# Two-layer hybrid decoder step on one core: group b's rows loaded ahead of the fourth weight, and one scale-and-bias of the last norm on GpSimd

## The chip, the cores and the metric

One core of one Trainium2 chip runs the whole program. The metric is device microseconds (us) of one execution; a median of three runs is given, and one further execution was recorded by the hardware profiler. The engines are TensorE (PE; its weight loads are listed apart as PEld), VectorE (DVE), ScalarE (ACT), GpSimd (POOL) and SyncE (SP), which issues most DMAs.

## The reference, cut to what matters

```
def reference(...):
    for i in range(2):                       # two layers
        if i == 0:   # sliding-window attention, 16 heads, rotary positions, sinks
            mp, kp, vp = swa_prompt(xp, w_qkv, b_qkv, sinks, w_o)       # 512 prompt rows
            ms, ks, vs = swa_sample(xs, cache_k, cache_v, ...)          # 8 sample rows
        else:        # gated linear attention on a matrix state
            mp, sp = gla_mix(xp, zeros, ...); ms, ss = gla_mix(xs, state_gla, ...)
        xp = layer_norm(ALPHA * xp + mp, ln_mix_g[i], ln_mix_b[i])
        xs = layer_norm(ALPHA * xs + ms, ln_mix_g[i], ln_mix_b[i])
        fp = conv_ffn(xp, ...); fs = conv_ffn(xs, ...)   # (gelu(conv3(x W_a)) * (x W_u)) W_down
        xp = layer_norm(ALPHA * xp + fp, ln_ffn_g[i], ln_ffn_b[i])
        xs = layer_norm(ALPHA * xs + fs, ln_ffn_g[i], ln_ffn_b[i])

def layer_norm(x, g, b):
    mu = mean(x); var = mean((x - mu) ** 2)
    return (x - mu) * rsqrt(var + 1e-5) * g + b
```

All is float32, with d_model 1024, 512 prompt rows and 8 sample rows.

## The kernel before

Activations lie transposed: a row of the model (1024 features) is spread over 128 partitions in 8 chunks (`KD`). The rows are split into group a (256 prompt rows) and group b (the other 256 and the 8 samples, 264 columns). `g.x` is a group's residual; `g.xh` and `g.xl` (for group a both in `xs_a`) are the high and low part of its rows for TensorE.

A weight matrix is worked off in units of 128 output columns: `load_unit` has SP load a unit into a `raw` tile (512 KB; `RAWS` = 2 such tiles, so that a load waits until the split of the unit two before it is done), ScalarE rounds it to the high part `wh` (L196), VectorE subtracts to get the low part `wl` (L202). `product` then runs 24 matmuls for one unit and one group: for each of 8 chunks high by high (L238), high weight by low rows (L240), low weight by high rows (L242). In the trace the results are tiles `accp`.

Units 0 and 1 are the keys and values of the attention layer, units 2 to 9 the queries, two heads of the 16 in each. After a query's product follow the rotation (`rope`: ScalarE `ra`, VectorE `rb`, GpSimd twice, L572 to L578), the split into `hl` (L623, L624), four small DMAs that rearrange it to `qs` (L628), scores against the keys (`sc`, L656, L657), softmax (L666 to L679), two transposes (`tp`, L685), two triangular cuts on GpSimd (`pu`, `pl`, L691) and the product with the values (`pv`, L704). The score tiles `sc` have two buffers. Then come the output projection (`out_proj`) and the norm (`ln_chunk`, `ln_end`), the feed-forward part, and the second layer with the gated linear attention.

`load_x` loads rows of a group into `g.x` and splits them: `xh` on ScalarE (L315), `xl` on VectorE (L316), one instruction of each per chunk. `attn_open` issues all loads of the start. Its loads on SP are under a manual schedule, in the order in which they are written. The order of the instructions on the other engines, and of SP later on, is set by a scheduler that estimates times when the program is built (`schedule_with_timeline_sim=True`). Every engine then works its own list strictly in that order.

The last norm of a group (`ln_end` with `last`) first gets its two sums from matmuls (L381, L383), then a short row of small steps on ScalarE and VectorE (L391 to L414), then goes over the 8 chunks in four pairs: VectorE multiplies a pair by the reciprocal deviation (L423), and each chunk is scaled and shifted by its own parameters: chunks 0, 1, 2, 4 and 6 on ScalarE (L426), chunk 3 on GpSimd (L428), chunks 5 and 7 on VectorE (L430). SP stores a pair when both are done (L437); of the last pair of group b, SP stores chunk 7 (L434) and ScalarE's queue chunk 6 (L435). `issue_after(behind)` holds a pair's multiplication behind the VectorE scaling of the pair before.

Of the kernel before, what the change touches and what calls it, by code (L numbers as in the profile page):

```python
# [82 lines left out]
def parted(rows):  # L83

    return rows.rearrange("p (j t) -> p t j", t=2)
# [15 lines left out]
class Net:  # L101
# [274 lines left out]
    def ln_end(self, g, i, last=False):  # L376
        nc, n, x = self.nc, g.n, g.x
        yield 0 if g.i and not last else 1
        e1, e2 = self.mtile("tp")[:, :n], self.mtile("pv")[:, :n]
        for e, sums, rest in ((e1, g.s1, x[:, KD - 1]), (e2, g.s2, g.q)) if last else ((e1, g.s1, None), (e2, g.s2, None)):  # L380
            nc.tensor.matmul(e, self.ones_a, sums, start=True, stop=rest is None)  # L381
            if rest is not None:
                nc.tensor.matmul(e, self.ones_a, rest, start=False, stop=True)  # L383
        t = lambda name, b=1: self.ln.tile([P, NT - 256], F32, name=name, bufs=b)[:, :n]
        mu, q, nv, r = t("mu"), t("msq"), t("nv"), t("r")
        banks = last or i % 2 == 0
        if banks:

            nv, vr = self.mtile("sc")[:, :n], self.mtile("sc")[:, :n]
        if last:  # L390
            self.square = nc.scalar.activation(q, e1, AF.Square).ins  # L391
            with self.tc.issue_after(self.square):
                nc.scalar.copy(mu, e1)
            for m in range(2, KD):
                nc.gpsimd.tensor_tensor(x[:, m], x[:, m], mu, op=ALU.subtract)
        else:
            self.square = nc.scalar.activation(q, e1, AF.Square).ins
        nvi = nc.vector.scalar_tensor_tensor(nv, q, LN_EPS, e2, op0=ALU.subtract, op1=ALU.subtract)

        with self.tc.issue_after(nvi.ins):  # L400
            for m in range(0, 2 if last else KD, 2):
                xp = x[:, m:m + 2]
                nc.vector.tensor_tensor(xp, xp, e1.unsqueeze(1).broadcast_to([P, 2, n]), op=ALU.subtract)
        nc.scalar.activation(r, nv, AF.Ln, scale=-1.0)
        self.exp = nc.scalar.activation(r, r, AF.Exp, scale=-0.5).ins
        if banks:
            nc.vector.tensor_tensor(vr, nv, r, op=ALU.mult)
            q = nv
            nc.vector.scalar_tensor_tensor(q, vr, 0.5, r, op0=ALU.mult, op1=ALU.mult)
        else:  # L410
            nc.vector.tensor_tensor(q, r, r, op=ALU.mult)
            nc.vector.scalar_tensor_tensor(q, q, 0.5, nv, op0=ALU.mult, op1=ALU.mult)
        rp = e2
        nc.vector.scalar_tensor_tensor(rp, q, 1.5, r, op0=ALU.add, op1=ALU.mult)  # L414
        sc = lambda m: self.par[:, C_LNG + i * KD + m:C_LNG + i * KD + m + 1]
        bi = lambda m: self.par[:, C_LNB + i * KD + m:C_LNB + i * KD + m + 1]
        if last:

            behind = None
            for m in range(0, KD, 2):  # L420
                xp = x[:, m:m + 2]
                with self.tc.issue_after(behind) if behind else ExitStack():
                    nc.vector.tensor_tensor(xp, xp, rp.unsqueeze(1).broadcast_to([P, 2, n]), op=ALU.mult)  # L423
                for j in (m, m + 1):
                    if j in (0, 1, 2, 4, 6):
                        nc.scalar.activation(x[:, j], x[:, j], AF.Identity, scale=sc(j), bias=bi(j))  # L426
                    elif j == 3:
                        nc.gpsimd.tensor_scalar(x[:, j], x[:, j], sc(j), bi(j), op0=ALU.mult, op1=ALU.add)  # L428
                    else:
                        behind = nc.vector.tensor_scalar(x[:, j], x[:, j], sc(j), bi(j), op0=ALU.mult, op1=ALU.add).ins  # L430
                y = lambda m0, m1: self.O["y"][:, m0:m1, g.c0:g.c0 + n]
                if g.i and m == KD - 2:

                    nc.sync.dma_start(out=y(m + 1, m + 2), in_=x[:, m + 1:m + 2])  # L434
                    nc.scalar.dma_start(out=y(m, m + 1), in_=x[:, m:m + 1])  # L435
                else:
                    nc.sync.dma_start(out=y(m, m + 2), in_=xp)  # L437
            return

        for m in range(KD):  # L440
            v = nc.vector.scalar_tensor_tensor(x[:, m], x[:, m], sc(m), rp, op0=ALU.mult, op1=ALU.mult)
            nc.scalar.activation(g.xh[:, m], parted(x[:, m]), AF.Identity, bias=bi(m))
            xl = nc.vector.scalar_tensor_tensor(g.xl[:, m], parted(x[:, m]), bi(m), g.xh[:, m].bitcast(F32), op0=ALU.add, op1=ALU.subtract)
        self.rest = xl.ins
        if g.i == 0:
            self.norm = self.slot + HOLD, self.exp, v.ins, xl.ins, self.next_phase() + 1
        if i % 2 == 0:
            if g.i:
                self.spawn(self.row_sums(i), 1)
            return  # L450
        for m in range(KD):
            yield 1 if m else LATEB
            self.shift(g, i, m)
# [66 lines left out]
    def attn_open(self):  # L520
        nc, I = self.nc, self.I
        self.ap, self.ap_cm = self.open("attn")
        p = self.ap
        t = lambda s, name, dt=F32: p.tile(s, dt, name=name)
        self.rope_t = t([P, 2, NT], "rope_t")
        self.mask0 = t([P, P], "mask0")
        self.own = t([P, 2, P], "own", I32)


        warm = self.acc.tile([P, 512], F32, name="accp")  # L530
        for _ in range(WARM):
            nc.tensor.matmul(warm[:, :P], self.ones_a, self.ones_a, start=True, stop=True)
        with self.tc.manual_schedule(engines={mybir.EngineType.SP}):
            r = self.raw.tile([P, KD * P], F32, name="raw")
            h, l = (self.wts.tile([P, KD * P], F32R, name=n) for n in ("wh", "wl"))
            for m in range(0, KD, 4):
                c = slice(m * P, m * P + 4 * P)
                nc.sync.dma_start(out=r[:, c], in_=I["w_qkv"][0][:, c])
                nc.gpsimd.tensor_scalar(h[:, c], r[:, c], 1.0, 0.0, op0=ALU.mult, op1=ALU.add)
                self.load_x(0, m, m + 2)  # L540
                nc.vector.tensor_tensor(l[:, c], r[:, c], h[:, c].bitcast(F32), op=ALU.subtract)
                self.load_x(0, m + 2, m + 4)
            self.w[0] = (h, l)
            self.load_unit(1, 4)
            nc.sync.dma_start(out=self.par, in_=I["par"])
            nc.sync.dma_start(out=self.rope_t[:, :, 0:256], in_=I["rope"][:, :, 0:256])
            nc.sync.dma_start(out=self.ident, in_=I["ident"])
            self.load_unit(2, 2)
            self.load_unit(3)
            for m in range(0, KD, 4):  # L550
                self.load_x(1, m, m + 4)
            nc.sync.dma_start(out=self.rope_t[:, :, 256:], in_=I["rope"][:, :, 256:])
            nc.sync.dma_start(out=self.mask0, in_=I["mask"])
            nc.sync.dma_start(out=self.own, in_=I["own"])
            for i in range(4, WSLOTS):
                self.load_unit(i)
        self.bq = t([P, KD], "bq")
        nc.vector.tensor_scalar(self.bq, self.par[:, C_BQKV + 2:C_BQKV + 10], 0.125, None, op0=ALU.mult)
        self.khi = [t([P, SEQ], f"khi{v}", F32R) for v in range(2)]
        self.klo = [t([P, SEQ], f"klo{v}", F32R) for v in range(2)]  # L560
        self.vtok = t([P, 4, P], "vtok")
        self.kc = t([P, NS, P], "kc")
        self.vc = t([P, NS, P], "vc")
        self.qz = t([P, NS * P], "qz")
        nc.gpsimd.memset(self.qz, 0.0)
# [947 lines left out]
```

## Time and profile before

| what | value |
|---|---|
| median of 3 runs | 1097.11 us (1095.06 to 1099.55) |
| the profiled execution's own time | 1094.2 us |
| its span, first to last instruction | 1092.5 us |
| mean granted TensorE clock | 0.997 |
| PE busy | 1059.4 us (97%) |
| DVE busy | 871.7 us (80%) |
| ACT busy | 683.4 us (63%) |
| POOL busy | 319.8 us (29%) |

A share of busy time is a mean over stages. The start (first loads), the attention (to about 143 us), the long feed-forward and second-layer part, and the end (the last norm of group b, after the last matmul) have to be read apart. Matmuls are pipelined, so that a busy PE may still be pausing: the distance between the starts of two matmuls tells more.

### The profile page before, as it was taken

What the parts mean: (1) busy time and instruction counts of PE and PEld (TensorE: products, weight loads), DVE (VectorE), ACT (ScalarE), POOL (GpSimd) and SP (SyncE); (2) the same over time, 40 slices, a digit from 0 to 9 for tenths busy, and PEclk for the clock granted to TensorE, in tenths of its full rate; (3) what the DMA queues carried; (4) which work ended last, traced back from release to release, by engine and by line L of the source; (5) the groups of instructions that cost most, each with busy time, mean ns of one, the idle gap of its engine ahead of it and who ended that gap; (6) DMA issues with size and microseconds to landing.
All of it is one profiled execution on the core that took longest, in us unless ns stands there. A gap on an engine that the chain in (4) does not pass through costs nothing. (4 is left out here: it accounts for less than half of the span.)

```text
span 1092.5 us, 23877 instructions
## 1 busy us (share of the span) xinstructions
PE 1059.4 (97%) x9174; PEld 1030.2 (94%) x9174; DVE 871.7 (80%) x1813; ACT 683.4 (63%) x1356; POOL 319.8 (29%) x512
## 2 busy tenths in 40 slices
PE   8999999999999999999999999989999999999996
PEld 8998899999999999999899999889999999999995
DVE  7898668988778878978767676588988788778975
ACT  5677657776655665547566656468776655665643
POOL 4576572221111110274321111363221111110263
PEclk9999999999999999999999999999999999999998
DMA  7454048587777774448235445368488777774322
GB/s 231 147 170 130 21 121 214 135 216 191 180 177 180 176 176 117 116 139 205 67 103 174 131 149 163 96 172 220 125 216 193 184 174 176 175 189 117 109 74 79
DMA packets 65474, 167.45 MB, mean 153 GB/s; under 512 B 8104, under 2 KB 28624, under 8 KB 65360
## 3 DMA queue, kind: packets, MB, share of 16 engines
q1 hardware_dynamic: 50960, 119.47, 33.8%
q0 software_dynamic: 12240, 44.57, 23.2%
q10 hardware_dynamic: 2160, 1.89, 0.5%
q8 instruction: 72, 1.18, 0.4%
q14 instruction: 42, 0.34, 0.1%
HBM read 153.24 MB, written 8.47 MB: 148 GB/s over the span
## 5 line engine op out<-in xcount | busy, mean ns | idle before, releaser
L315 ACT ACTIVATE wh<-raw 128x1024 fp32r<-128x1024 f32 x72 | 76.0, 1058 | 89.9 <-PE widep L929 44.7
L196 ACT ACTIVATE wh<-raw 128x1024 fp32r<-128x1024 f32 (+1 forms) x92 | 96.2, 1047 | 41.4 <-PE accp L240 14.5
L311 PE MATMUL widep<-tl,wh 128*128 128x264 f32 (+1 forms) x432 | 119.1, 276 | 0.0
L312 PE MATMUL widep<-th,wl 128*128 128x264 f32 (+1 forms) x432 | 119.1, 276 | 0.0
L310 PE MATMUL widep<-th,wh 128*128 128x264 f32 (+1 forms) x432 | 119.1, 276 | 0.0
L238 PE MATMUL accp<-xh_b,wh 128*128 128x264 f32 x400 | 112.9, 282 | 2.7 <-DVE hprod L823 2.7
L242 PE MATMUL accp<-xh_b,wl 128*128 128x264 f32 x400 | 111.4, 279 | 0.0
L208 POOL DMA_DIRECT2D wl<-in_w_down x28 | 24.2, 866 | 291.8 <-ACT wl L207 269.1
L238 PE MATMUL accp<-xs_a,wh 128*128 128x256 f32 x400 | 105.5, 283 | 4.0 <-ACT wh L196 3.3
L240 PE MATMUL accp<-xl_b,wh 128*128 128x264 f32 x384 | 107.0, 279 | 0.0
L240 PE MATMUL accp<-xs_a,wh 128*128 128x256 f32 x384 | 102.5, 282 | 0.0
L316 DVE TENSOR_TENSOR wl<-raw,wh 128x1024 fp32r<-128x1024 f32 x72 | 87.7, 1221 | 7.0 <-ACT wh L315 7.0
L202 DVE TENSOR_TENSOR wl<-raw,wh 128x1024 fp32r<-128x1024 f32 (+2 forms) x64 | 78.8, 1239 | 14.3 <-ACT wh L196 13.0
L207 ACT ACTIVATE wl<-wh 128x1024 fp32r<-128x1024 f32 x85 | 89.0, 1051 | 0.9
L310 PEld LDWEIGHTS widep<-th,wh 128*128 128x128 f32 x432 | 82.1, 190 | 0.0
L311 PEld LDWEIGHTS widep<-tl,wh 128*128 128x128 f32 x432 | 82.1, 190 | 0.0
L312 PEld LDWEIGHTS widep<-th,wl 128*128 128x128 f32 x432 | 82.1, 190 | 0.0
L238 PEld LDWEIGHTS accp<-xs_a,wh 128*128 128x128 f32 x400 | 76.5, 194 | 5.5 <-ACT wh L196 3.8
L238 PEld LDWEIGHTS accp<-xh_b,wh 128*128 128x128 f32 x400 | 75.7, 189 | 4.7 <-DVE hprod L823 3.5
L310 PE MATMUL widep<-xh_b,wh 128*128 128x264 f32 x288 | 79.6, 276 | 0.0
L311 PE MATMUL widep<-xl_b,wh 128*128 128x264 f32 x288 | 79.5, 276 | 0.0
L312 PE MATMUL widep<-xh_b,wl 128*128 128x264 f32 x288 | 79.5, 276 | 0.0
(423 smaller groups left out, 4008.7 us busy)
## 6 DMA issues: line engine op xcount, KB each, us to landing
raw<-in_w_up SPq DMA_DIRECT2D x88, 512.0 KB, 4.0
wl<-in_w_up POOLq DMA_DIRECT2D x52, 512.0 KB, 6.9
raw<-in_w_down SPq DMA_DIRECT2D x44, 512.0 KB, 3.6
wl<-in_w_down POOLq DMA_DIRECT2D x28, 512.0 KB, 6.5
raw<-in_w_gla SPq DMA_DIRECT2D x24, 512.0 KB, 3.5
raw<-in_w_mix_o SPq DMA_DIRECT2D x16, 512.0 KB, 4.1
qs<-hl SPq DMA_DIRECT2D x64, 64.0 KB, 2.1
sgla<-in_state_gla SPq DMA_DIRECT2D x16, 256.0 KB, 3.1
```

What stands on the lines that cost most here:

```text
L196: nc.scalar.activation(h[:, c], r[:, c], AF.Copy)
L202: nc.vector.tensor_tensor(l[:, c], r[:, c], h[:, c].bitcast(F32), op=ALU.subtract)
L207: self.nc.scalar.activation(l, h.bitcast(F32), AF.Copy, scale=-1.0)
L208: self.nc.gpsimd.dma_start(out=l, in_=src, accum_op=ALU.add)
L238: nc.tensor.matmul(o, h[:, ks], xh, start=k == 0, stop=False)
L240: nc.tensor.matmul(o, h[:, ks], xl, start=False, stop=False)
L242: nc.tensor.matmul(o, l[:, ks], xh, start=False, stop=not tail and k == nt - 1)
L310: self.nc.tensor.matmul(o, h[:, ks], rh, start=k == 0, stop=False)
L311: self.nc.tensor.matmul(o, h[:, ks], rl, start=False, stop=False)
L312: self.final = self.nc.tensor.matmul(o, l[:, ks], rh, start=False, stop=k == KD // 2 - 1).ins
L315: self.nc.scalar.activation(hi, src, AF.Copy)
L316: self.nc.vector.tensor_tensor(lo, src, hi.bitcast(F32), op=ALU.subtract)
```

## The change

Two edits. In `attn_open` the two loads of group b's rows (`load_x(1, ...)`, 528 KB each) are issued before the load of unit 3 (512 KB, the second unit of queries) and no longer behind it. In the last norm of group b alone (`g.i` is 1) chunk 5's scale and bias go to GpSimd.

```
             self.load_unit(2, 2)
-            self.load_unit(3)
             for m in range(0, KD, 4):
                 self.load_x(1, m, m + 4)
+            self.load_unit(3)
...
-                    elif j == 3:
+                    elif j == 3 or j == 5 and g.i:
                         nc.gpsimd.tensor_scalar(x[:, j], x[:, j], sc(j), bi(j), op0=ALU.mult, op1=ALU.add)
```

Because the scheduler orders the program anew, the first edit changes the order on every engine through the whole attention, up to the first steps of the output projection; behind that, the lists of the two kernels are the same but for tile numbers, until the end.

**ScalarE at the start.** `raw_167` or `raw_185` is unit 3, `xh_b` the high part of group b's rows, `ra_311` the rotation's first step for unit 2. Before:

```order
L590 ACTIVATE khi1_210<-rr_249 64x256
L196 ACTIVATE wh_168<-raw_167 128x1024
L315 ACTIVATE xh_b_90<-x_b_89 128x264 x4
L572 ACTIVATE ra_311<-accp_286,bq_207 128x256
L315 ACTIVATE xh_b_90<-x_b_89 128x264 x4
L572 ACTIVATE ra_356<-accp_331,bq_207 128x256
```

and after:

```order
L590 ACTIVATE khi1_210<-rr_249 64x256
L315 ACTIVATE xh_b_90<-x_b_89 128x264 x8
L572 ACTIVATE ra_311<-accp_286,bq_207 128x256
L196 ACTIVATE wh_186<-raw_185 128x1024
L196 ACTIVATE wh_195<-raw_194 128x1024
L623 ACTIVATE hl_319<-rr_317 128x256
```

The high part of unit 3 moves from ahead of the eight splits of group b's rows to behind them.

**TensorE at the same place.** `accp_286` is unit 2 for group a, `accp_331` unit 3 for group a, `accp_403` unit 0 (the keys) for group b. Before:

```order
L242 MATMUL accp_286<-xs_a_87,wl_160 128x256
L238 MATMUL accp_331<-xs_a_87,wh_168 128x256
L240 MATMUL accp_331<-xs_a_87,wh_168 128x256
L238 MATMUL accp_403<-xh_b_90,wh_112 128x264
L242 MATMUL accp_331<-xs_a_87,wl_169 128x256
```

and after:

```order
L242 MATMUL accp_286<-xs_a_87,wl_160 128x256
L238 MATMUL accp_331<-xs_a_87,wh_186 128x256
L240 MATMUL accp_331<-xs_a_87,wh_186 128x256
L238 MATMUL accp_403<-xh_b_90,wh_112 128x264
L240 MATMUL accp_403<-xl_b_91,wh_112 128x264
L242 MATMUL accp_403<-xh_b_90,wl_113 128x264
```

Two matmuls of unit 3 still stand ahead of group b's first product, which is now worked through in one piece.

**GpSimd at the end of the attention.** L356 are the subtractions of group a's first norm, L691 the cuts of group b's last heads. Before:

```order
L691 AFFINE_SELECT pu_2023<-pt_2021 128x256
L691 AFFINE_SELECT pl_2024<-pt_2021 128x256
L356 TENSOR_TENSOR x_a_86<-x_a_86,sa_2067 128x256 x7
L691 AFFINE_SELECT pu_2088<-pt_2086 128x256
L691 AFFINE_SELECT pl_2089<-pt_2086 128x256
L374 TENSOR_TENSOR s2_a_2077<-s2_a_2077,sq_2113 128x256
L691 AFFINE_SELECT pu_2097<-pt_2095 128x256
L691 AFFINE_SELECT pl_2098<-pt_2095 128x256
```

and after:

```order
L356 TENSOR_TENSOR x_a_86<-x_a_86,sa_2067 128x256 x5
L691 AFFINE_SELECT pu_2023<-pt_2021 128x256
L691 AFFINE_SELECT pl_2024<-pt_2021 128x256
L356 TENSOR_TENSOR x_a_86<-x_a_86,sa_2067 128x256 x2
L374 TENSOR_TENSOR s2_a_2077<-s2_a_2077,sq_2113 128x256
L691 AFFINE_SELECT pl_2089<-pt_2086 128x256
L691 AFFINE_SELECT pl_2098<-pt_2095 128x256
L691 AFFINE_SELECT pu_2088<-pt_2086 128x256
L691 AFFINE_SELECT pu_2097<-pt_2095 128x256
```

Five of the seven subtractions move ahead of the cuts of the last head but one. On TensorE the last `pv` product, which needs the cuts at the end of this list, stands behind 1 matmul of the output projection of group b in the new order, and stood behind 21 of its 24 before.

## Rows read from the trace of the kernel before

**Rows 1.** Windows, 60 to 80 us: length, busy PE, PEld, DVE, ACT, POOL, PEclk, DMA, GB/s.

```profile
60.00:80.00 20.00, 19.68 (x177) 18.81 (x178) 19.77 (x56) 15.03 (x46) 14.75 (x22) 1.00 0.45 139
```

**Rows 2.** Timeline, PE at the start: start us, us, line, tiles [idle before <-releaser].

```profile
17.67 0.38 PE L238 MATMUL accp<-xs_a,wh 128*128 128x256 f32 x1 [0.49 <-ACT wh L196]
...
18.93 0.38 PE L242 MATMUL accp<-xs_a,wl 128*128 128x256 f32 x1 [0.55 <-DVE wl L202]
...
25.11 0.38 PE L238 MATMUL accp<-xs_a,wh 128*128 128x256 f32 x1 [0.65 <-ACT wh L196]
```

**Rows 3.** Timeline, ACT at the start.

```profile
16.56 1.06 ACT L196 ACTIVATE wh<-raw 128x1024 fp32r<-128x1024 f32 x1
17.52 1.46 ACT L315 ACTIVATE xh_b<-x_b 128x264 fp32r<-128x264 f32 x4
18.86 0.49 ACT L572 ACTIVATE ra<-accp,bq 128x256 f32<-128x256 f32 x1
19.22 1.66 ACT L315 ACTIVATE xh_b<-x_b 128x264 fp32r<-128x264 f32 x4
```

**Rows 4.** View of tile `x_b`, 0 to 30 us: count, ns min/median/max, first and last start.

```profile
L315 ACT ACTIVATE xh_b<-x_b x8: 427/482/525, 17.5 to 20.4; 128x264 fp32r<-128x264 f32 x8
```

**Rows 5.** An issue of SP at the start; DMA view, median us from issue to landing.

```profile
18.90 0.33 SPq L191 DMA_DIRECT2D raw<-in_w_qkv  x1
...
raw<-in_w_qkv SPq DMA_DIRECT2D x4, 512.0 KB, 4.6
...
qs<-hl SPq DMA_DIRECT2D x6, 64.0 KB, 2.7
```

**Rows 6.** Timeline, DVE at the start.

```profile
30.91 1.23 DVE L202 TENSOR_TENSOR wl<-raw,wh 128x1024 fp32r<-128x1024 f32 x1 [1.59 <-ACT wh L196]
```

**Rows 7.** Waits of PE, 38 to 143 us: in total, times, longest; first and last of eight.

```profile
PE sc L656 <- ACT pr L673: 1.6, 3, 0.7
...
PE accp L240 <- DVE hl_b L744: 0.2, 1, 0.2
```

**Rows 8.** Timeline, end of the attention: POOL, and PE's last value product.

```profile
128.08 5.60 POOL L356 TENSOR_TENSOR x_a<-x_a,sa 128x256 f32<-128x256 f32 x7 [0.39 <-ACT sa L353]
...
135.77 0.40 POOL L691 TENSOR_SCALAR_AFFINE_SELECT pl<-pt 128x256 f32<-128x256 f32 x1
...
137.74 0.44 PE L704 MATMUL pv<-pl,vtok 128*64 128x128 f32 x4
```

**Rows 9.** Timeline from 1084.8 us: the last norm's pairs, and the store of chunk 7.

```profile
1086.82 0.42 DVE L430 TENSOR_SCALAR x_b<-x_b,par 128x264 f32<-128x264 f32 x1
1087.15 0.70 DVE L423 TENSOR_TENSOR x_b<-x_b,pv 128x528 f32<-128x528 f32 x1
...
1085.59 2.10 ACT L426 ACTIVATE x_b<-x_b,par 128x264 f32<-128x264 f32 x4 [2.20 <-DVE x_b L423]
1087.88 0.61 ACT L426 ACTIVATE x_b<-x_b,par 128x264 f32<-128x264 f32 x1 [0.19 <-DVE x_b L423]
...
1086.28 0.56 POOL L428 TENSOR_SCALAR x_b<-x_b,par 128x264 f32<-128x264 f32 x1
...
1088.33 0.38 SPq L434 DMA_DIRECT2D out_y<-x_b  x1
```

**Rows 10.** DMA view, 1080 to 1093 us: GB/s in 40 slices of 0.325 us.

```profile
GB/s 0 0 0 0 0 0 0 0 25 0 0 0 0 0 0 0 0 0 0 0 0 0 0 182 328 374 331 383 322 367 361 357 306 16 0 0 0 0 0 0
```

**Rows 11.** Windows behind the last matmul; PE's matmuls before and after 10.3 us.

```profile
1081.61:1085.40 3.79, 0.00 (x0) 0.00 (x0) 2.92 (x6) 1.03 (x3) 3.49 (x5) 1.00 0.01 2
1085.60:1086.00 0.40, 0.00 (x0) 0.00 (x0) 0.40 (x1) 0.40 (x1) 0.40 (x1) 0.50 0.00 0
...
5.59 0.55 PE L238 MATMUL accp<-xs_a,wh 128*128 128x256 f32 x1 [0.74 <-ACT xs_a L315]
9.77 0.42 PE L240 MATMUL accp<-xs_a,wh 128*128 128x256 f32 x1
10.92 0.28 PE L240 MATMUL accp<-xs_a,wh 128*128 128x256 f32 x1
```

More of the change, by code (lines that the diff above doesn't have):

```diff
@@ L426, in ln_end @@
                         nc.scalar.activation(x[:, j], x[:, j], AF.Identity, scale=sc(j), bias=bi(j))
-                    elif j == 3:
+                    elif j == 3 or j == 5 and g.i:
                         nc.gpsimd.tensor_scalar(x[:, j], x[:, j], sc(j), bi(j), op0=ALU.mult, op1=ALU.add)
@@ L548, in attn_open @@
             self.load_unit(2, 2)
-            self.load_unit(3)
             for m in range(0, KD, 4):
                 self.load_x(1, m, m + 4)
+            self.load_unit(3)
             nc.sync.dma_start(out=self.rope_t[:, :, 256:], in_=I["rope"][:, :, 256:])
```

## The prediction

> **What bounds the kernel now.** I read the busy shares first, then the windows by stage, then the start and the end in the timelines. TensorE works 97% of the span. In the attention (to about 143 us) it isn't alone: from 60 to 80 us it is busy 19.68 of 20 us and VectorE 19.77 [rows 1], so either being late would show, and neither has much room to catch up there. The 177 matmuls of that window give 0.111 us for one matmul in a full stream. Behind 143 us the lists of both kernels are alike, so what the attention gains or loses is carried to the end as it is. After the last matmul the last norm of group b is a chain of its own. Both edits have to be judged in their stages: the load at 12 to 30 us and what it does to the order as far as 143 us, the norm's edit behind 1086 us.
>
> At the start TensorE waits three times: 0.49 us for unit 3's high part, 0.55 for its low part, 0.65 for unit 5's high part [rows 2]. The high part of unit 3 is made at 16.56 us, the moment ScalarE has got through the keys; the eight splits of group b's rows follow it [rows 3]. No instruction is listed as waiting for group b's rows to land [rows 4]: when ScalarE comes to them they are there. So the thing that is loaded earlier is not the thing that anyone waits for; ScalarE's turn is.
>
> **The change part by part. First the hole on TensorE.** In the new order ScalarE does all eight splits and the first step of unit 2's rotation before unit 3's high part, and TensorE, whose next matmuls are still those of unit 3, has to wait for it. From 16.56 us: four splits 1.34 us (17.52 to 18.86), four more 1.66, the rotation's step 0.36 (18.86 to 19.22), the high part 1.06 [rows 3], together 4.4, so it ends at 21.0 us and not at 17.6. TensorE goes on at 21.0 and not at 17.67: **+3.4 us**. If all splits came at the pace of the first four (0.335) it would be +3.0; at the recorded length of one (0.482 [rows 4]) +4.2. The load itself doesn't matter here: unit 3's needs the raw tile of unit 1 in either order.
>
> **Then the waits that go.** The 0.55 and 0.65 us [rows 2] have no place in the new order: behind the two matmuls comes group b's whole product (24 matmuls, 2.7 us), which covers unit 3's low part, and unit 5 is used some 80 matmuls later. With the refilling of the pipeline, about 0.1 each: **-1.4 us** (-1.2 to -1.6).
>
> **A wait that may come.** The scores of unit 2 now stand 53 matmuls behind unit 3's first, and stood 98 behind it. TensorE is there at 21.0 + 53 x 0.111 = 26.9 us. VectorE ends unit 3's subtraction at 21.0 + 1.2 = 22.2 [rows 6]; then come the rest of the rotation and the split, three small steps on three engines (1.5 us, an estimate from steps of 0.4 to 0.7 us), two issues of `qs` ahead of the one that matters (1.2) and its landing (2.7 [rows 5]): 27.6. **+0.7 us**, between 0 and 1.5.
>
> **VectorE.** Unit 5's load waits for that same subtraction, on SP, with the `qs` transfers queued behind it. It is issued at 22.2 us, not at 18.90, and lands 4.6 us later [rows 5] at 26.8; ScalarE's step makes it 27.9, and VectorE, which does its list in order, stands still from about 24. TensorE needs it only at about 31. In place of it VectorE loses most of the 1.59 us that it waited before unit 6 [rows 6]; unit 6, issued behind the four `qs` at about 26, lands at 30.7 and can be subtracted from 31.8 us, not 30.91, with half a us more of other work done. VectorE is 0.4 to 0.9 us late.
>
> So at about 36 us TensorE is 3.4 - 1.4 + 0.7 = 2.7 us late, VectorE under 1. From 38 to 143 us TensorE's waits come to 5.4 us in eight rows, nearly all for the softmax chain or for its results [rows 7]. Where TensorE waits for the chain, its own lateness costs nothing. Of the 2.7 us I carry half: **+1.3 us**, between 0.4 (VectorE's alone) and 2.7.
>
> **The end of the attention.** GpSimd's seven subtractions of group a's norm take 5.60 us, and the last cut is made by 136.2 us; the last value product starts 1.6 us later, at 137.74 [rows 8]. In the new order two more cuts lie inside that stretch (0.8 us), so the last cut comes about 0.8 later after its start. The value product stands 20 matmuls earlier on TensorE, so these 2.2 us of work come behind it instead of covering the wait, and cover the step to the next operand (0.5). **+0.3 us**, from 0 to 2.3.
>
> **The last norm.** VectorE's chunk 5 (0.42 us) leaves the path: the last pair's multiplication can start at 1086.8 and not at 1087.15 [rows 9]. GpSimd has done chunk 3 by 1086.84 and takes 0.56, so chunk 5 is ready at 1087.4; chunk 4 of the same pair keeps ScalarE until 1087.69, so the pair's store isn't later. ScalarE's chunk 6 moves from 1087.88 to 1087.6, chunk 7 by about 0.4; its store, issued at 1088.33, stands behind the store of the pair before. But from 1087.6 to 1090.7 us the transfers are at 306 to 383 GB/s throughout [rows 10], for all the stores of group b together: the last ones queue there anyway. **-0.2 us**, between -0.45 and 0.
>
> **Sum.** 1.3 + 0.3 - 0.2 = +1.4 us. The profiled execution took 1094.2 us in all (span 1092.5, 1.7 around it); it becomes 1095.6. The median of the runs lies 2.9 us above it, so the forecast is **1098.5 us**.
>
> **Rival 1: nothing comes of it.** The hole is wholly taken up by the waits behind it, and the rest is as said: 1097. For it: the chain's waits [rows 7] are twice the lateness. Against it: both engines are full at 60 to 80 us [rows 1].
>
> **Rival 2: the chain runs ahead.** Scores asked for 45 matmuls sooner start the softmax sooner, and TensorE's 5.4 us of waits [rows 7] shrink. Half of them gone and the hole with them: -2.7 - 0.2, 1094.2. All of them gone, 1091.5. For it: the second pair of heads, too, is asked for earlier by the new list (after 131 matmuls and not after 154). Against it: VectorE, on which that chain rests, starts no earlier.
>
> **Rival 3: the clock falls in the hole, and the kernel is slower.** Behind the last matmul the granted clock stays at 1.00 for 3.8 us of idle TensorE and is 0.50 from then on, 1.2 in place of 2.4 GHz [rows 11]. The hole is 3.8 us of idle (0.49 + 3.4), just there. At the start TensorE worked from 5.59 to 10.3 us at the lower level, one matmul recorded with 0.42 us and then 0.28 [rows 11]: 4.7 us that lose between a third (1.6) and a half (2.4). A slow TensorE has no waits to hide in, so all is carried: 2.7 + 2.4 + 0.3 - 0.2 = +5.2, 1102.3; with the wait for the scores at its upper end 1103.1. It decides once the hole is longer than the idle stretch that the clock bears, and is worth over 0.5% if the lower level lasts as long as at the start. Against it: the hole may be 3.5 as well. The Trainium skill (TensorE: Matmul & The Clock Gate, Part 1: The HAM clock gate) says that the array is throttled by default and that only recent activity keeps the throttle off, so that an idle stretch is paid for twice; that speaks against this change. By that rule the time would be this rival's; the fall in the rows agrees with it, and no run here shows one in the middle of the kernel.
>
> **Rival 4: GpSimd holds up the end of the attention.** The 2.7 us are carried whole, and the value product waits for the cuts with nothing to cover it (2.3): +4.8, 1101.9, and more if the subtractions start late.
>
> **How the numbers follow.** Forecast 0.45, rival 1 0.18, rival 2 0.17, rival 3 0.12, rival 4 0.08. About 0.5% (5.5 us) is what a measurement of this kernel can tell from no change. Over 5.5 us faster is the far part of rival 2: 0.07. Over 5.5 slower are 0.08 of rival 3 and 0.05 of rival 4: 0.13. The rest, 0.80, is within. The range 1093 to 1103 leaves out the far part of rival 2 and the upper ones of rivals 3 and 4, nearly 2 in 10. The rescheduled softmax stretch from 38 to 143 us, for which no row has a price, sets its width.
>
> **What would show it.** TensorE's timeline: one idle of 3 to 4 us before the third query product's first matmul at about 21 us, and no wait behind it until the scores. VectorE: idle of 3 to 4 us before unit 5's subtraction at about 28. The windows: clock 1.00 from 10.3 us to the end of the matmuls (rival 3 is wrong) or 0.50 behind 20 us. The start of the last value product (137.74 before [rows 8]) tells what was carried. At the end: the last pair's multiplication 0.35 us sooner, the last store hardly. I am wrong if TensorE doesn't idle at 21 us, or if the stretch from 38 to 143 us changes by over 4 us by itself.

## The result, and the profile after

| | before | after |
|---|---|---|
| median of the timed runs, us | 1097.60 (1094.43 to 1099.55) | 1106.22 (1102.53 to 1108.89) |
| ratio after to before, 95% interval | 1 | 1.0081 (1.0066 to 1.0096) |
| the profiled execution's own time, us | 1094.2 | 1107.05 |
| its span, us | 1092.5 | 1105.3 |
| mean granted clock of that span | 0.997 | 0.988 |

The change makes the kernel slower by 0.8%, some 8.9 us. The forecast was 1098.5 us, with a range from 1093 to 1103. The two profiled executions differ by 12.8 us of span, more than the medians do: the one of before is among its fastest runs, the one of after lies close to its median.

**The start.** Timeline of after, TensorE and then ScalarE; columns are start, length, engine, line, operation, and in brackets the idle time before it and what ended it (answers to [rows 2, 3]):

```profile
16.67 0.28 PE L242 MATMUL accp<-xs_a,wl 128*128 128x256 f32 x1
20.50 0.38 PE L238 MATMUL accp<-xs_a,wh 128*128 128x256 f32 x1 [3.56 <-ACT wh L196]
...
16.32 2.83 ACT L315 ACTIVATE xh_b<-x_b 128x264 fp32r<-128x264 f32 x8
19.05 0.45 ACT L572 ACTIVATE ra<-accp,bq 128x256 f32<-128x256 f32 x1
19.41 1.04 ACT L196 ACTIVATE wh<-raw 128x1024 fp32r<-128x1024 f32 x1
```

The hole is there: TensorE's first matmul of unit 3 is at 20.50 us, 2.83 later than before, behind the eight splits and the rotation's step. The other two waits of [rows 2] are gone.

**The clock.** Windows of after, TensorE alone: the window and its length, TensorE's busy time and matmuls, the granted clock (1.00 is 2.4 GHz, 0.50 is 1.2 GHz; a mean of 0.51 comes of the window's edges), the DMA share and GB/s. (The answers to [rows 11]; before has 1.00 in all of these places. A stretch is placed to about 0.1 us.)

```profile
21.20:24.60 3.40, 3.40 (x18) 0.51 0.35 110
24.60:38.00 13.40, 13.07 (x116) 1.00 0.48 146
140.70:147.50 6.80, 6.31 (x34) 0.51 0.11 29
147.50:160.00 12.50, 11.98 (x104) 1.00 0.29 85
536.60:540.00 3.40, 3.40 (x18) 0.51 0.46 154
741.40:744.80 3.40, 3.40 (x17) 0.51 0.13 25
```

The clock falls four times before the last matmul. The first fall is right behind the hole. The second, the longest, lies at the end of the attention, where no single wait is long. The other two stand behind waits that before has as well (2.13 us at 527 us, 1.76 at 730; here 2.58 and 1.93) without a fall in its profile.

**The end of the attention.** Timeline of after: GpSimd (answers to [rows 8]), and the two matmuls of TensorE that open the sums of the norm for group a and for group b, which I use as landmarks; then the same two matmuls in before. Below it all waits of TensorE from 126 to 143 us (who waited for whom: us in total, times, longest):

```profile
130.67 3.85 POOL L356 TENSOR_TENSOR x_a<-x_a,sa 128x256 f32<-128x256 f32 x5 [0.82 <-ACT sa L353]
134.48 0.59 POOL L691 TENSOR_SCALAR_AFFINE_SELECT pu<-pt 128x256 f32<-128x256 f32 x1
135.03 0.59 POOL L691 TENSOR_SCALAR_AFFINE_SELECT pl<-pt 128x256 f32<-128x256 f32 x1
135.58 1.59 POOL L356 TENSOR_TENSOR x_a<-x_a,sa 128x256 f32<-128x256 f32 x2
...
129.29 0.38 PE L347 MATMUL sc<-x_a,ones_a 128*128 128x256 f32 x1
148.86 0.49 PE L347 MATMUL sc<-x_b,ones_a 128*128 128x264 f32 x1 [0.52 <-DVE x_b L343]
```

```profile
126.21 0.42 PE L347 MATMUL sc<-x_a,ones_a 128*128 128x256 f32 x1
140.79 0.49 PE L347 MATMUL sc<-x_b,ones_a 128*128 128x264 f32 x1 [0.52 <-DVE x_b L343]
```

```profile
PE accp L238 <- ACT hh_b L740: 1.1, 1, 1.1
PE pv L736 <- DVE hl_b L316: 1.0, 1, 1.0
PE tp L730 <- ACT pt L687: 0.8, 1, 0.8
PE pv L704 <- POOL pl L691: 0.6, 1, 0.6
PE tp L685 <- DVE pts L732: 0.4, 1, 0.4
PE pv L704 <- DVE hl_b L744: 0.4, 1, 0.4
```

In before the two sums start at 126.21 and 140.79 us. So after is 3.1 us late when group a's sum comes, and the stretch between the sums takes 19.57 us and not 14.58: another 5.0. The cuts wait behind five subtractions. The value products (`pv`) have one buffer, so each waits for the split of the one before it (L316, L744), and in the new list almost nothing stands between them. The waits are short (0.4 to 1.1 us), but they come one after another, and about the end of the fifth of the six the clock falls, at 140.7 us.

**The rest.** From group b's sum to the last sum of the kernel before takes 940.2 us and after 944.5. The two falls at 536 and 741 us, reckoned at half of their 3.4 us each, are 3.4 of these 4.3. Such falls are not the change's alone: ten of the thirteen other profiles have one or two between 160 us and the last matmul; before's has none. The end behind the last sum takes 11.53 us before and 11.94 after. Together 3.1 + 5.0 + 4.3 + 0.4 = 12.8 us, the span's 12.8.

### The profile page after: what moved, and what is told of

The parts are those of the page before. It is cut to its first block, busy times and chain, and to the rows that moved or that the text cites. A ratio compares the mean times of both kernels' runs of the same rounds, so it can differ in the third digit from the quotient of the medians.

```text
span 1105.3 us, 23887 instructions
## 1 busy us (share of the span) xinstructions
PE 1064.7 (96%) x9174; PEld 1035.6 (94%) x9174; DVE 871.3 (79%) x1812; ACT 683.1 (62%) x1356; POOL 311.5 (28%) x513
## 5 line engine op out<-in xcount | busy, mean ns | idle before, releaser
L196 ACT ACTIVATE wh<-raw 128x1024 fp32r<-128x1024 f32 (+1 forms) x92 | 96.1, 1047 | 41.3 <-PE accp L240 17.7
L316 DVE TENSOR_TENSOR wl<-raw,wh 128x1024 fp32r<-128x1024 f32 x72 | 87.7, 1220 | 7.0 <-ACT wh L315 7.0
```

Of the source, the lines that this page charges most:

```text
L196: nc.scalar.activation(h[:, c], r[:, c], AF.Copy)
L316: self.nc.vector.tensor_tensor(lo, src, hi.bitcast(F32), op=ALU.subtract)
```

## The experiments

To undo an order without undoing the loads, the lists of all engines were fixed: behind the program's last line each engine's instructions are chained in the order of a table. The table holds the list of before, that of after, or the one as far as a point and the other behind it. The changed lists fall into three parts: the start (to about 37 us), the middle (to about 120 us) and the end of the attention.

```
-        Net(tc, ctx, I, O).run()
+        net = Net(tc, ctx, I, O)
+        net.fills = []
+        net.run()
+        pinned(tc, net.fills)
...
+        for one, two in zip(row, row[1:]):
+            tc.add_manual_dep(two, one.name, mybir.DependencyInfo(mybir.DependencyClass.NoSync, mybir.DependencyReason.DATA), reason="pinned")
```

All results together. "Hole" is TensorE's wait ahead of unit 3; "a" and "b" are the starts of the two sums; "low clock" gives the stretches at 1.2 GHz near the hole and near the end of the attention, in the one profiled execution of each. The ratio is to before, run on the same chip.

| kernel | median us | ratio, 95% interval | hole | a | b | b - a | low clock, 19 to 27 | low clock, 133 to 151 |
|---|---|---|---|---|---|---|---|---|
| before | 1096.0 to 1097.6 | 1 | 0.49 | 126.21 | 140.79 | 14.58 | - | - |
| norm_only | 1097.97 | 1.0009 (0.9996 to 1.0021) | 0.36 | 126.44 | 142.68 | 16.24 | - | 135.9 to 139.3 |
| order_back | 1099.70 | 1.0030 (1.0015 to 1.0044) | 2.75 | 130.15 | 146.31 | 16.16 | 19.7 to 26.5 | 139.1 to 142.6 |
| order_back_fill | 1098.74 | 1.0028 (1.0016 to 1.0040) | filled | 128.26 | 144.51 | 16.25 | - | 138.0 to 141.4 |
| seg_abb | 1100.10 | 1.0037 (1.0023 to 1.0052) | 3.53 | 129.50 | 144.06 | 14.56 | 21.7 to 25.2 | - |
| seg_aab | 1100.60 | 1.0046 (1.0028 to 1.0065) | 3.53 | 131.27 | 145.84 | 14.57 | 19.3 to 26.1 | - |
| after | 1106.22 | 1.0081 (1.0066 to 1.0096) | 3.56 | 129.29 | 148.86 | 19.57 | 21.2 to 24.6 | 140.7 to 147.5 |
| end_new | 1103.05 | 1.0057 (1.0038 to 1.0076) | 0.48 | 127.34 | 146.30 | 18.96 | - | 137.5 to 144.3 |
| end_pool | 1104.61 | 1.0080 (1.0060 to 1.0100) | 3.54 | 129.43 | 149.54 | 20.11 | - | 141.7 to 148.5 |
| end_pe | 1109.99 | 1.0124 (1.0102 to 1.0146) | 3.68 | 129.04 | 154.71 | 25.67 | 21.3 to 24.7 | 133.9 to 140.8, 144.2 to 151.0 |
| fill_21 | 1102.12 | 1.0057 (1.0037 to 1.0077) | 0.31 | 127.67 | 147.27 | 19.60 | - | 139.1 to 146.0 |
| fill_141 | 1102.05 | 1.0046 (1.0030 to 1.0063) | 3.90 | 129.55 | 146.44 | 16.89 | 20.4 to 23.8 | - |
| fill_both | 1100.50 | 1.0033 (1.0019 to 1.0048) | 0.24 | 128.15 | 145.04 | 16.89 | - | - |
| before_fill | 1094.89 | 0.9984 (0.9971 to 0.9998) | 0.48 | 126.27 | 140.84 | 14.57 | - | - |

### One edit alone: the last norm

The kernel before, with `elif j == 3 or j == 5 and g.i:` in place of `elif j == 3:`.

> Only the last norm's edit; loads and lists of the attention as before. Every theory that puts the loss into the attention: 1097 us, ratio to before 0.999 to 1.001, and the end of the profile no shorter than before by over 0.3 us. If the norm's edit carries part of the 8.6 us lost: over 1100.

No difference that can be measured: 1.0009, from 0.9996 to 1.0021. So the loss comes with the other edit. But the end did not get shorter. From the first pair's multiplication to the last instruction it takes 7.65 us before and 8.24 here (8.42 in after). The windows behind that multiplication, VectorE alone, first before (it starts at 1084.85), then norm_only (1087.76), then after (1096.92):

```profile
1090.20:1090.72 0.52, 0.00 (x0) 0.50 0.97 327
1090.72:1092.50 1.78, 0.00 (x0) 0.50 0.01 3
```

```profile
1093.10:1093.62 0.52, 0.00 (x0) 0.50 0.95 333
1093.62:1096.00 2.38, 0.00 (x0) 0.50 0.01 2
```

```profile
1102.30:1102.80 0.50, 0.00 (x0) 0.50 0.97 338
1102.80:1105.34 2.54, 0.00 (x0) 0.50 0.01 1
```

The transfers end 5.87, 5.86 and 5.88 us behind the multiplication: the stores are bound by the transfers, whoever scales chunk 5. What is left behind them is 0.6 to 0.8 us longer with the edit. There SP issues the last store and ScalarE's queue the one ahead of it, in before the other way round. No row says what these 0.6 us are, and it was not tried to swap the two.

### The loads alone: all lists of before

> Both edits stay, group b's rows are loaded ahead of unit 3, but every engine is held to the list of the kernel before (GpSimd's chunk 5 at the end excepted). Theory O, the loss comes through the new lists: 1097 us, ratio 0.998 to 1.002, TensorE's wait for unit 3's high part 0.5 to 1 us, clock 1.00 at 21 and at 141 us. Theory T, the earlier transfer itself costs (it holds up what stands behind it on SP's queue): over 1101, with the loss visible by 37 us.

Neither theory had it. 1.0030 is slower than before, but only some 3 us of the 8.9, and the hole is there: 2.75 us, with ScalarE's old list. The timeline of this kernel, SP's issue of unit 3's load, ScalarE's split and TensorE, and below it the window behind (0.50 is the clock):

```profile
12.19 0.34 SPq L191 DMA_DIRECT2D raw<-in_w_qkv  x1
...
18.77 1.06 ACT L196 ACTIVATE wh<-raw 128x1024 fp32r<-128x1024 f32 x1 [2.07 <-DMA raw<-in_w_qkv]
...
19.88 0.58 PE L238 MATMUL accp<-xs_a,wh 128*128 128x256 f32 x1 [2.75 <-ACT wh L196]
```

```profile
19.80:26.40 6.60, 6.28 (x27) 0.50 0.28 89
```

and SP's issue of the same load in before:

```profile
12.25 0.33 SPq L191 DMA_DIRECT2D raw<-in_w_qkv  x1
```

The load is issued at the same time in both, since it waits for the raw tile. But with group b's 1056 KB ahead of it in the transfers it lands 6.6 us after its issue, at 18.75 us, and ScalarE waits for it; in before it lands after 3.5 us, at 15.75, where ScalarE did not wait for it [rows 3]. This is a step of the prediction that failed ("The load itself doesn't matter here"). In after the load lands 5.7 us after its issue, at 17.7 us, and ScalarE comes to it only at 19.41, so there the new list sets the length of the hole, as predicted. The late landing is a shorter cause behind it, which shows once the list is put back. The other way round, ScalarE's new list with the loads of before, was not run. The Trainium skill (DMA: Bandwidth & Descriptors, "Two DMAs through the same engine are not ordered") says that descriptors of one queue start in order on a DMA engine; the landing 3.0 us later agrees with it.

To see what the clock has to do with it, the hole was filled with 11 matmuls of ones, into the tile that unit 3's product then overwrites:

```
+    mm = lambda n, at: net.fills.append(([net.nc.tensor.matmul(ps[:, :P], net.ones_a, net.ones_a, start=True, stop=True).ins for _ in range(n)], at))
+    if u == 3 and not g.i:
+        mm(11, 82)
```

> As the run with the loads of the changed kernel and all lists of before (1099.7, ratio 1.003), with 11 matmuls of ones in the hole that unit 3's late weights leave (2.4 of the 2.75 us). Theory C, more than half of that run's 3.3 us is the clock's fall behind the hole: ratio 1.001 to 1.0015, clock 1.00 at 19 to 27 us. Theory H, it is the hole itself: 1.003, unchanged, although the clock stays up.

1.0028 against 1.0030: theory H by the times. The clock stays up from 19 to 27 us, and in the profiles group a's sum comes 1.9 us sooner (128.26 against 130.15), yet the medians don't show it. Of the 12 runs of order_back the two with a mean clock of 0.997 took 1095.9 and 1096.5 us, the six with 0.990 or 0.991 took 1098.4 to 1102.7, so the falls seem not to come in each run. How much of these 3 us is the clock stays open.

### Adding the new lists part by part

The new list of the start alone, and then start and middle, each with the old lists behind:

> Both edits stay. The lists of the changed kernel are kept as far as about 37 us (ScalarE does the eight splits ahead of unit 3's high part); behind that every engine follows the list of the kernel before. Theory L, the start's list is what costs: 1104 or more, over 4 us above the run with all lists of before (1099.7). Theory T, the start's loss is the landing of unit 3's weights behind group b's rows, which both lists wait for: 1099 to 1101, no different from 1099.7 by over 1.5 us.

> Both edits stay. The lists of the changed kernel as far as about 120 us, and from there (GpSimd's last cuts ahead of group a's subtractions, 20 matmuls of group b's product ahead of the last value product) those of the kernel before. Theory E, the order at the end of the attention costs 4 to 5 us with the clock's fall that it brings: 1101 to 1102, ratio 1.004. Theory M, the softmax stretch from 38 to 120 us is what costs: 1105 or more, ratio over 1.007, with the sum of group a's first chunk at 129 us as in the changed kernel.

The ladder reads 1.0030 (old lists), 1.0037 (new start), 1.0046 (new start and middle), 1.0081 (all new). Theory T holds for the start: its new list costs no more than the late landing did. Theory E holds for the end: the last part alone is worth 0.0035, 3.8 us (the two intervals just miss each other). The middle, from 38 to 120 us, adds about 1 us, less than the intervals tell apart. With the old end the stretch between the sums is 14.56 and 14.57 us again, in spite of the hole and of a fall at 20 us ahead of it.

The end on its own, on the kernel before with the norm's edit:

> Loads and lists of before as far as about 120 us, then the lists of the changed kernel to the end of the attention (and its last norm). No hole at the start. Theory E, the new end costs by itself: 2.3 us, or 5 with the clock's fall, in the stretch from group a's sum to group b's (16.9 to 19.6 us, before 14.6): ratio 1.003 to 1.0045. If the end only costs because the start made the kernel late: under 1.0015.

1.0057: theory E, and rather more than expected. There is no hole and the clock is 1.00 from 11 to 137 us, but the waits of after's end stand there one by one (0.97 us ahead of the sample's value product, 0.94 ahead of group b's product), and the clock falls from 137.5 to 144.3. The end needs no late start.

### Filling TensorE's waits

The changed kernel with its own lists; matmuls of ones in the hole, in the waits at the end of the attention, and in both:

```
+    if u == 3 and not g.i:
+        mm(15, 82)
+    if u == 10 and g.i:
+        mm(2, 839)
+    if u == 10 and g.i:
+        mm(4, 871)
+    if u == 10 and g.i:
+        mm(4, 959)
```

> The changed kernel, every engine held to its own list, with 15 matmuls of ones added in the hole on TensorE ahead of unit 3 (about 3.2 us of the 3.56 idle). The granted clock should then stay at 1.00 at 21 to 25 us. Theory C1, the fall behind the hole is carried to the end: 1104 to 1105 us, 1.5 to 2 less than the changed kernel. Theory C0, the waits of the softmax chain take it up: 1106, the same within 1 us, and the second group of scores at 37.5 us as in the changed kernel.

> The changed kernel, held to its own list, with 2, 4 and 4 matmuls of ones added in TensorE's waits at 135, 137 and 140 us (0.4, 0.9 and 0.9 us, each shorter than the wait that it stands in). Theory C, the fall of the clock from 140.7 to 147.5 us costs 3.4 us: clock 1.00 from 126 to 160 us and 1102.8, ratio 1.005. Theory O alone (the order at the end of the attention, not the clock): 1106, ratio 1.008, although the clock stays up.

> The changed kernel, held to its own list, with the 15 matmuls of ones in the hole at 17 us and the 10 at 135 to 140 us. Singly they gave 1102.1 and 1102.1, 4 us less than the changed kernel's 1106.2. Theory C, two falls of the clock, each with its own cost: 1098 to 1100, ratio 1.002 to 1.004, clock 1.00 from 15 to 160 us. Theory of one cost (the second fall only comes because the first made the kernel late): about 1102, as with one of them.

The windows of fill_21 behind the hole, of fill_141 at the end of the attention, and of fill_both over both places:

```profile
20.90:26.20 5.30, 5.30 (x48) 1.00 0.31 100
```

```profile
126.00:143.00 17.00, 14.98 (x141) 1.00 0.01 1
143.00:160.00 17.00, 16.48 (x144) 1.00 0.32 105
```

```profile
15.00:30.00 15.00, 13.45 (x117) 1.00 0.57 186
126.00:160.00 34.00, 31.46 (x281) 1.00 0.22 59
```

Added work makes the kernel faster: 1.0081 becomes 1.0057, 1.0046 and 1.0033 (the first interval still touches that of after, the other two don't). The filled kernels are also held to their lists, which after is not. No run holds them without fillers; the nearest is end_pool below, which is held too, differs only in GpSimd's cuts and takes 1.0080.

For the end theory C holds. The clock stays up there, and the stretch between the sums is 16.89 us, twice, against 19.57 and, in before, 14.58: 2.3 us are the waits of the new list, the other 2.7 the clock. A filler both shortens a wait and adds work for TensorE, so these runs don't tell whether the clock falls for the waits or for the small products between them.

For the hole the runs don't decide between C1 and C0. TensorE's scores of unit 2 in after and in fill_21, then ScalarE's waits from 81 to 95 us in after, fill_21 and end_pool:

```profile
28.21 0.29 PE L656 MATMUL sc<-khi,qs 128*128 128x256 f32 x1
28.24 0.39 PE L656 MATMUL sc<-khi,qs 128*128 128x256 f32 x1 [1.24 <-DMA qs<-hl]
```

```profile
83.94 0.42 ACT L623 ACTIVATE hl<-rr 128x256 fp32r<-128x256 f32 x1 [1.99 <-DMA qs<-hl]
93.01 0.42 ACT L623 ACTIVATE hl<-rr 128x256 fp32r<-128x256 f32 x1 [3.13 <-DMA qs<-hl]
...
82.84 0.42 ACT L623 ACTIVATE hl<-rr 128x256 fp32r<-128x256 f32 x1 [0.65 <-DMA qs<-hl]
91.89 0.42 ACT L623 ACTIVATE hl<-rr 128x256 fp32r<-128x256 f32 x1 [2.66 <-DMA qs<-hl]
...
83.32 0.42 ACT L623 ACTIVATE hl<-rr 128x256 fp32r<-128x256 f32 x1 [1.15 <-DMA qs<-hl]
93.06 0.42 ACT L623 ACTIVATE hl<-rr 128x256 fp32r<-128x256 f32 x1 [3.80 <-DMA qs<-hl]
```

With the new lists TensorE gets back at once what it loses at the low clock behind the hole: at full clock it reaches the scores sooner, but waits there 1.24 us for `qs` to land. The second group of scores comes at 37.28 us in fill_21 and 37.49 in after, the sign set for C0, and to 82 us the two keep within 0.3 us of each other. Only behind that do they part: after is 1.1 us the later one by 95 us and 1.6 at group a's sum (129.29 against 127.67). Most of that comes from 83 to 94 us, where ScalarE waits longer for the landings of `qs`. end_pool has the hole open and no fall behind it, and its sum is as late, 129.43. So these profiles do not put the 1.6 us down to the fall. Why the landings differ no run shows. By the times the hole's filler gains in one pair only so much that the intervals touch, and in the others less (fill_141 to fill_both 1.0046 to 1.0033, order_back to its filled form 1.0030 to 1.0028).

Both fillers together are worth 0.0048, 5.3 us; the 3.6 that fill_both is still slower than before are the late start and the new end at full clock (1.9 and 2.3 in its profile). The mean clocks of all timed runs point to the clock too: span times (1 - mean clock) averages 14.0 us for after, 11.0 for fill_21, 9.0 for fill_141, 6.0 for fill_both, and 6.9 for 24 runs of before. The difference of 7.1 between after and before is an upper bound, since a low clock costs nothing while TensorE waits.

### Which list at the end

First GpSimd's cuts alone put back, then TensorE's list alone:

> The changed kernel, every engine held to its own list but GpSimd at the end of the attention: the two cuts that stood among group a's subtractions go ahead of all seven again, the last four in the order of before. Theory G, the late cuts are what holds TensorE up: the 0.56 us wait at 135.7 goes and the waits behind it start earlier, 1103 to 1104. Theory P, TensorE's own list is at fault (short products in a row, each waiting for the one before): 1105 to 1106, the waits of 0.97 and 1.14 us ahead of the sample's value product and of group b's product stay.

> The changed kernel, every engine held to its own list but TensorE from 131 us to the last value product: there the list of before (a value product first, then group a's 24 matmuls, then the sample's values, then 20 matmuls of group b ahead of the last value product). GpSimd still makes the cuts late. Theory P: the 24 and the 20 matmuls cover the waits, the stretch from group a's sum to group b's takes 15 to 16 us and not 19.6, 1102. Theory G: the first of these value products now waits 3 to 3.5 us for the late cuts with nothing ahead of it, the gain is eaten up and the clock falls all the same: 1105 to 1107.

GpSimd alone: 1.0080, no gain. TensorE's waits from 126 to 145 us in end_pool:

```profile
PE accp L238 <- ACT hh_b L740: 1.1, 1, 1.1
PE pv L736 <- DVE hl_b L316: 1.0, 1, 1.0
PE accp L238 <- DVE x_a L343: 0.8, 1, 0.8
```

The two longest stay, as theory P has it, and the wait for the cut is replaced by one for VectorE, 0.8 us. TensorE alone: 1.0124, the slowest of all, as theory G has it and by more than it said. GpSimd's cut and TensorE in end_pe:

```profile
135.39 0.70 PE L704 MATMUL pv<-pl,vtok 128*64 128x128 f32 x4 [3.59 <-POOL pl L691]
...
134.75 0.59 POOL L691 TENSOR_SCALAR_AFFINE_SELECT pl<-pt 128x256 f32<-128x256 f32 x1
```

TensorE stands for 3.59 us before a cut that GpSimd makes at 134.75, and the clock falls twice. So neither list is at fault by itself: the new list of TensorE is the one that suits late cuts, the old one suits early cuts, and of the orders that were run only that of before, on all engines, covers the waits. The old lists of these two engines together, with the others new, were not run.

### A version that is faster than both

The same cure on the kernel before, with its own loads, norm and lists: 2 matmuls of ones ahead of group b's first output product, 9 in the wait at 527 us, 7 in the one at 730 us.

```
+    if u == 72 and not g.i:
+        mm(9, 4329)
+    if u == 10 and g.i:
+        mm(2, 959)
+    if u == -2 and not g.i:
+        mm(7, 5841)
```

> The kernel before, held to its own list, with matmuls of ones in three of TensorE's waits: 2 ahead of group b's first output product (0.54 us of wait), 9 ahead of a product of the second layer (2.13 us at 527 us), 7 ahead of a sum of a norm (1.76 us at 730 us). Theory C, the spread of the kernel before (1094.1 to 1099.8) is falls of the clock behind such waits: 1 to 2 us less than before, ratio 0.998 to 0.999, and the spread smaller. If the falls come from elsewhere, or the added matmuls delay: 0.9995 to 1.002.

0.9984 (0.9971 to 0.9998): 1094.89 us against 1097.41, faster than before by under 0.2%, barely clear of no difference, and so faster than after. Its windows, TensorE alone:

```profile
126.00:160.00 34.00, 32.02 (x275) 1.00 0.25 68
520.00:545.00 25.00, 24.57 (x201) 1.00 0.20 65
714.60:718.10 3.50, 3.37 (x14) 0.51 0.25 80
720.00:750.00 30.00, 30.00 (x263) 1.00 0.81 205
```

No fall where the fillers stand, and one at 714.6 us behind waits of 1.16 and 0.62 us that were left alone. That the spread gets smaller did not come true: 1091.1 to 1096.6 us here, 1093.4 to 1099.5 in before beside it. Nor is it shown that the gain is the clock's: span times (1 - mean clock) averages 6.5 us here and 7.0 in before beside it.

## Why the prediction was wrong

- **The hole, +3.4.** Right in place and cause, and close in size: 2.83. A second, shorter cause behind it, the late landing of unit 3, was denied with a wrong reason: that the load is issued at the same time in either order says nothing on when it lands.
- **The waits that go, -1.4, and the score wait, +0.7.** Right: the two waits are gone. The wait for the scores is there at full clock, 1.24 us in fill_21 and 1.33 in end_pool, inside the range of 0 to 1.5; in after, where the clock falls first, it is gone too, and up to the second group of scores TensorE waits only once, for 0.33 us.
- **Half carried, +1.3 (0.4 to 2.7).** With the hole filled it is 1.5 and 1.9 us at group a's sum (fill_21, fill_both), inside the range; in after 3.1, above it. Rival 3, held at 0.12, named a fall of the clock, and the fall came, in six of the seven profiles with a hole of 2.75 to 3.9 us left open and in none of the seven without one. The Trainium skill's rule quoted there (TensorE: Matmul & The Clock Gate, Part 1) agrees with that; the row that it was weighed against, 3.8 us at full clock behind the last matmul [rows 11], was read as if a hole a little shorter were nearly safe. But the rival's other step, "A slow TensorE has no waits to hide in, so all is carried", failed: the wait for the scores at 28 us took the loss up. The 1.6 us by which after is later than fill_21 come behind 82 us, most of them where ScalarE waits for `qs` at 83 to 94 us, and end_pool has them without a fall; their cause stays open.
- **The end of the attention, +0.3 (0 to 2.3).** This is the term that failed: at full clock the stretch between the sums grows by 2.3 us, the upper end, and as it ran by 5.0. I priced the last value product alone, and asked what covers its wait. The new list has two value products and between them the sample's, all on one `pv` buffer, with one matmul of group b between the last two, and each of them waits. And I looked for a fall of the clock only behind a long idle stretch. Here the longest wait is 1.14 us; a stretch with a row of short ones was enough. With the new end unfilled (its two mixed forms counted in) the clock fell in five of five profiles; with the old end left as it is in three of six, each time for half as long, and not in before_fill, where one of its waits is filled; with the new end filled in none of two. The Trainium skill (TensorE: Matmul & The Clock Gate, "A second HAM failure mode: psum-queue depth-cycling") tells of a kernel with bf16 matmuls in which small pauses between groups of matmuls, frequent enough, bring the clock down and up again. The trace here has one such fall, 0.51 from 140.70 to 147.50 us.
- **The last norm, -0.2 (-0.45 to 0).** That the transfers bind the end was right. In the profiles the sign was wrong, since 0.6 us came behind the last transfer, where I had looked for nothing.
- **The rest of the kernel, taken as alike.** The lists are alike, but in after's profile the two falls at 536 and 741 us add some 3.4 us. Most of the other profiles have such falls too, so this part is chance of one execution as far as is known.
- **The cases.** Rivals 3 and 4 were given chances as if only one of them could come true. The fall of the one and the uncovered end of the other both came. Rival 3's 1102.3 with the uncovered end at 2.3 in place of 0.3 is 1104.3; with the second fall's 2.7 it is 1107.0, close to what after took, but in part by luck, since rival 3's price of the first fall is not what the profiles show. What the forecast described is the change at full clock, and there (fill_both) it costs 3.6 us and not 1.4: most of that error is the end of the attention, 2.3 and not 0.3.

## What to carry to other kernels

A wait on the engine that bounds the kernel can have a second price, a fall of its clock: here over half of the loss (5.3 of 8.9 us) went when idle TensorE was given useless matmuls, and the profiles let 2.7 us of it be followed to one fall. Look for it not only behind one long hole but wherever several short waits stand close together, and read the clock by windows before anything else. Then follow the loss to the next wait: the 2.7 us at the end of the attention stayed; what was lost behind the hole was, with the new lists, gone by the next wait for a transfer. And when a scheduler answers an edit with new lists, undo them in parts, all engines together: one engine's list put back alone gained nothing here (GpSimd) or made it worse (TensorE).

## What the runs showed of the hardware that was not expected

- The clock fell in a stretch whose longest wait was 1.14 us, and not always: the same lists of before gave it at 135.9 to 139.3 us in one profile (norm_only) and not in that of before. Where it came at the old end, the stretch between the sums grew from 14.57 to 16.2 us.
- A load of 512 KB issued at 12.0 to 12.3 us landed after 3.5 us (before), or after 5.7 and 6.6 (after, order_back) with 1056 KB of other loads issued ahead of it.
- Behind the last transfer the program still takes 1.78 us in before, and 2.38 to 2.54 in norm_only and after, where SP issues the last store and ScalarE's queue the one before it; that the issuer is the cause was not tested.
